# Down projection as seven block products, with two of the weight sums made by accumulating transfers

## The chip, the cores and the metric

The kernel runs on one core of a Trainium2 chip. The metric is the device time of one execution in microseconds; lower is better. TensorE multiplies and adds into PSUM, VectorE and ScalarE work on SBUF and PSUM, GpSimd on SBUF; SP issues nearly all transfers, each engine works through its own queue in order, and engines wait for each other by semaphores.

## The reference: what is computed

A decoder layer on 512 tokens of width 1024: RMSNorm, three token mixers (two of attention, one state space model) with gates, a projection back, a residual; then RMSNorm, a gated feed-forward with a short convolution, a residual, and a last RMSNorm. The change is in the feed-forward and the last norm:

```python
def conv_ffn(h, w_up, conv_w, conv_b, w_down):
    up = h @ w_up                                  # (512, 1024) @ (1024, 5632)
    up = conv_general_dilated(up, conv_w, ...) + conv_b   # 3 taps, per channel
    gate, val = split(up, 2)
    return (silu(gate) * val) @ w_down             # (512, 2816) @ (2816, 1024)
x = x + conv_ffn(rmsnorm(x, norm_ffn), ...)
out = rmsnorm(x, norm_final)
```

## The kernel before

All arithmetic is float32. TensorE multiplies in a shorter format, so each operand is split into a high part (a copy made by ScalarE into that format, L66) and a low part (the difference, made by VectorE, L92 for weights), and each product is three matmuls: high x high, high x low, low x high (`mm3m`, L177 to L179).

The order of all work is written by hand. `units` is a list of steps, each with the weight chunk that it uses; `run` goes through it, and before each step it emits the splits of the next chunk, whatever `plan` has for that step (`before(u, ...)`) and what the step before left in `later`. A chunk is loaded by SP into one of two `raw` buffers of 1 MB; its pieces of 128 x 1024 are split into `whi` and `wlo`, four buffers each, so a split waits for TensorE to be done with the piece four before it.

The up stage takes the 22 blocks of 128 channels two at a time, c = 0 to 10. For each c there are four steps of 24 matmuls (gate and value, two blocks each). ScalarE and VectorE do the convolution of each result in the tile `cc`, ScalarE the silu, VectorE the product; ScalarE and VectorE split the product into `gh[f]` and `gl[f]`, 128 channels x 512 tokens.

The down stage (`down_unit`) computes the output in two halves of 512 columns. In each it goes through the 22 channel blocks in six chunks (2, 4, 4, 4, 4, 4), with four accumulators in PSUM, one for each 128 tokens: 2 x 22 x 4 x 3 matmuls. When the first half ends, `residual` adds the four results to `x1`, ScalarE sums squares, and GpSimd multiplies by the final norm's weights (`gfin`). In the second half the accumulators end one after another; for the last 128 tokens the last four blocks are done in two pieces of 256 columns (`fin`), so that the end after the last matmul is short. `finish` makes the power -0.5 on GpSimd, scales the two halves on ScalarE and VectorE, and SP stores each.

Of the kernel before, what the change touches and what calls it, by code (L numbers as in the profile page):

```python
# [31 lines left out]
def hybrid_block(  # L32
# [167 lines left out]
    def run(first, live):  # L200
# [14 lines left out]

        def split_to(ci, n):
# [10 lines left out]
            if done[ci] == len(c.defs):  # L227
                load_to(ci + 3)
# [914 lines left out]
    gfin = []  # L1143

    def load_gfin():
        gfin.append(hp_.tile([128, DM], F32, tag="hTh", name="gfin"))
# [4 lines left out]
    def down_unit(chunk, half, k0, n):
        def fn():
            if k0 == 0:
                for t in range(NT):
                    acc[t] = bank(DTAG[half][t], name="acc")
            order = [(t, k) for k in range(n) for t in range(NT)]
            whole = slice(0, 512)
            if k0 + n == NF:
                order = [(t, k) for t in range(NT) for k in range(n)]
                if half == 1:  # L1160
                    order = order[:-n]
            order = [(t, k, whole) for t, k in order]
            final = k0 + n == NF and half == 1
            if final:

                order += [(NT - 1, k, c) for c in (slice(0, 256), slice(256, 512)) for k in range(n)]
                fin = {0: bank("sc", name="fin"), 256: bank("pt", name="fin")}
            for t, k, c in order:
                o = slice(t * 128, t * 128 + 128)
                kk = k0 + k  # L1170
                w = tuple(v[:, c] for v in chunk.get(k))
                if final and t == NT - 1:
                    ps, starts, stops = fin[c.start][:, 0:256], k == 0, k == n - 1
                else:
                    ps = acc[t]
                    starts, stops = kk == 0, kk == (NF - 5 if half == 1 and t == NT - 1 else NF - 1)
                mm3m(ps, gh[kk][:, o], gl[kk][:, o], w, starts, stops)
                if not stops:
                    continue
                if kk < NF - 1:  # L1180
                    y = x1[t // 2][:, t % 2, 512:1024]
                    tt(y, y, ps, ADD)
                    continue
                if half == 0:
                    residual(t, half, acc[t], fss)
                    row = x1[t // 2][:, t % 2, whole]
                    stt(fss[:, 8 + t:9 + t], fss[:, t:t + 1], 1.0 / DM, epsv, MUL, ADD)
                    tt(row, row, gfin[0][:, whole], MUL, G)
                    continue
                y, oc = x1[t // 2][:, t % 2, 512 + c.start:512 + c.stop], cc[0][:, t, c]  # L1190
                ss = fss[:, 4 + t:5 + t] if c.start == 0 else fss[:, 12:13]
                tt(y, y, ps, ADD)
                S.activation(ps, y, AF.Square, accum_out=ss)
                for f in rest[:1] if final and t == NT - 1 else rest[:]:
                    rest.remove(f)
                    f()
                tt(oc, y, gfin[0][:, 512 + c.start:512 + c.stop], MUL, G if t < NT - 2 else V)
                parts.append(ss)
                if c.stop == 512:
                    for ss in parts:  # L1200
                        ms = fss[:, 8 + t:9 + t]
                        stt(ms, ss, 1.0 / DM, ms, MUL, ADD)
                    parts.clear()
                    finish(t)
# [4 lines left out]
    def finish(t):
        ms, row, y = fss[:, 8 + t:9 + t], x1[t // 2][:, t % 2, 0:512], cc[0][:, t, :]  # L1210
        G.tensor_tensor(ms, ms, mhalf, op=ALU.pow)

# [4 lines left out]
        def second():
            ts(y, y, ms, MUL)
            SY.dma_start(out[0, t * 128:(t + 1) * 128, 512:1024], y)

        rest.extend((first, second))
# [195 lines left out]
```

## Time and profile before

| | before |
|---|---|
| median of 3 runs | 832.57 us (831.45 to 832.61) |
| profiled execution, its own time | 834.41 us |
| profiled execution, its span | 832.6 us |
| TensorE busy | 815.8 us, 98% |
| VectorE, ScalarE, GpSimd busy | 470.8, 363.3, 160.1 us |
| up stage, down stage | to 705.8 us, then to 825.6 us |

The span runs from the first to the last instruction that the profiler saw. A line number such as L92 is that of the source; where a helper issues an operation, it is the helper's. Matmuls overlap: one of 512 columns shows 389 ns, but the next starts earlier. "PEld" is TensorE's load of the stationary operand.

### The profile page before, as it was taken

The numbers are of one execution on the slowest core, as the hardware profiler recorded it, in microseconds if no ns is written. First come the engines' busy times: TensorE is split into PE (matmuls) and PEld (weight loads), VectorE is DVE, ScalarE is ACT, GpSimd is POOL, SyncE is SP. The second block draws the span as 40 slices with busy tenths as digits, with TensorE's granted clock in tenths as the row PEclk, the third lists the DMA queues.
The fourth block names the chain that finished last, engine by engine and source line by source line (L and its number), as shares of the span: only waits on it lengthen the run. The fifth ranks groups of instructions, "written<-read, shape, count | busy, mean of one in ns | idle before, by whom it ended". The sixth has DMA issues, their size and how long they took to land.

```text
span 832.6 us, 10517 instructions
## 1 busy us (share of the span) xinstructions
PE 815.8 (98%) x4085; PEld 677.2 (81%) x4085; DVE 470.8 (57%) x913; ACT 363.3 (44%) x673; POOL 160.1 (19%) x217
## 2 busy tenths in 40 slices
PE   8999899999999999999999999999999999999996
PEld 7978778778787888888878998888888888888885
DVE  7998666674636638272755466655566555423313
ACT  6446556457354546242443354444444444313212
POOL 6199623523200100032610000000000000002002
PEclk9999799999999999999999999999999999999998
DMA  9332131132331122332261313333333323412402
GB/s 248 96 103 62 40 102 52 51 95 46 63 106 52 53 78 76 102 102 70 93 245 51 99 52 102 101 102 102 101 102 102 101 77 102 167 60 77 152 0 102
DMA packets 68277, 76.60 MB, mean 92 GB/s; under 512 B 8160, under 2 KB 55556, under 8 KB 68228
## 3 DMA queue, kind: packets, MB, share of 16 engines
q1 hardware_dynamic: 67972, 75.89, 28.7%
q8 instruction: 32, 0.52, 0.3%
q0 software_dynamic: 256, 0.05, 0.1%
q14 instruction: 17, 0.14, 0.1%
HBM read 73.81 MB, written 2.12 MB: 91 GB/s over the span
## 4 chain that ended last, share of the span: by engine, by line
PE 84%; DVE 8%; DMA 2%; ACT 2%; issue 1%; POOL 1%; SPq 1%; POOLq 0%; DVEq 0%; ACTq 0%
PE mm L171 10%; PE up L172 10%; PE up L171 10%; PE up L173 10%; PE mm L172 9%; PE mm L173 9%; PE acc L178 6%; PE acc L179 6%; PE acc L177 6%; DVE wlo L92 1%; DVE us L624 1%; PE sc L895 1%; PE sc L763 1%; PE sc L684 1%; PE o L722 1%
## 5 line engine op out<-in xcount | busy, mean ns | idle before, releaser
L92 DVE TENSOR_TENSOR wlo<-raw,whi 128x1024 fp32r<-128x1024 f32 (+1 forms) x126 | 150.3, 1203 | 152.5 <-ACT whi L66 152.4
L66 ACT ACTIVATE whi<-raw 128x1024 fp32r<-128x1024 f32 (+1 forms) x126 | 127.3, 1023 | 58.4 <-PE acc L179 56.2
L171 PE MATMUL up<-hTh,whi 128*128 128x512 f32 (+1 forms) x384 | 142.7, 372 | 0.0
L172 PE MATMUL up<-hTl,whi 128*128 128x512 f32 (+1 forms) x384 | 142.6, 371 | 0.0
L173 PE MATMUL up<-hTh,wlo 128*128 128x512 f32 (+1 forms) x384 | 142.6, 371 | 0.0
L171 PE MATMUL mm<-hTh,whi 128*128 128x512 f32 (+1 forms) x336 | 133.5, 397 | 0.0
L172 PE MATMUL mm<-hTl,whi 128*128 128x512 f32 (+1 forms) x336 | 130.5, 388 | 0.0
L173 PE MATMUL mm<-hTh,wlo 128*128 128x512 f32 (+1 forms) x336 | 130.3, 388 | 0.0
L275 DVE SCALAR_TENSOR_TENSOR cc<-up,cpar,cc 128x511 f32<-128x511 f32 x88 | 65.9, 749 | 97.3 <-ACT cc L1107 95.8
L171 PEld LDWEIGHTS up<-hTh,whi 128*128 128x128 f32 x384 | 72.3, 188 | 12.6
L173 PEld LDWEIGHTS up<-hTh,wlo 128*128 128x128 f32 x384 | 72.3, 188 | 12.5
L172 PEld LDWEIGHTS up<-hTl,whi 128*128 128x128 f32 x384 | 72.3, 188 | 12.3
L171 PEld LDWEIGHTS mm<-hTh,whi 128*128 128x128 f32 x336 | 64.2, 191 | 14.7 <-issue 2.5
L173 PEld LDWEIGHTS mm<-hTh,wlo 128*128 128x128 f32 x336 | 63.9, 190 | 13.1
L172 PEld LDWEIGHTS mm<-hTl,whi 128*128 128x128 f32 x336 | 63.9, 190 | 11.8
L178 PE MATMUL acc<-wlo,gh 128*128 128x512 f32 x172 | 66.9, 389 | 0.0
L179 PE MATMUL acc<-whi,gl 128*128 128x512 f32 x172 | 66.9, 389 | 0.0
L177 PE MATMUL acc<-whi,gh 128*128 128x512 f32 x172 | 66.9, 389 | 0.0
L279 POOL TENSOR_TENSOR x<-x,gfin 128x512 f32<-128x512 f32 x4 | 5.2, 1290 | 296.8 <-ACT acc L1046 296.8
L1107 ACT ACTIVATE cc<-up,cpar 128x512 f32<-128x512 f32 x44 | 34.3, 779 | 61.2 <-PE up L173 60.4
L989 ACT ACTIVATE th<-mm 128x512 f32<-128x512 f32 x24 | 14.3, 595 | 67.3 <-PE mm L173 67.3
L66 ACT ACTIVATE gh<-cc 128x512 fp32r<-128x512 f32 x22 | 13.9, 632 | 59.4 <-DVE cc L279 59.4
(297 smaller groups left out, 1271.4 us busy)
## 6 DMA issues: line engine op xcount, KB each, us to landing
raw<-in_w_up_dram SPq DMA_DIRECT2D x22, 1024.0 KB, 5.1
raw<-in_w_in_dram SPq DMA_DIRECT2D x18, 1024.0 KB, 5.1
raw<-in_w_down_dram SPq DMA_DIRECT2D x10, 1024.0 KB, 5.0
x<-in_x_dram SPq DMA_DIRECT2D x8, 512.0 KB, 6.1
raw<-in_w_in_dram SPq DMA_DIRECT2D x8, 512.0 KB, 5.4
raw<-in_w_out_dram SPq DMA_DIRECT2D x4, 1024.0 KB, 5.0
raw<-in_w_branch_a_dram SPq DMA_DIRECT2D x4, 512.0 KB, 5.9
raw<-in_w_branch_c_dram SPq DMA_DIRECT2D x2, 1024.0 KB, 5.0
```

The source lines that it names most:

```text
L66: S.activation(o, i, AF.Copy)
L92: (lo_eng or V).tensor_tensor(view(lo), r, view(hi).bitcast(F32), op=ALU.subtract)
L171: PE.matmul(ps, wh, xh, start=first, stop=False)
L172: PE.matmul(ps, wh, xl, start=False, stop=False)
L173: PE.matmul(ps, wl, xh, start=False, stop=last)
L177: PE.matmul(ps, xh, wh, start=first, stop=False)
L178: PE.matmul(ps, xh, wl, start=False, stop=False)
L179: PE.matmul(ps, xl, wh, start=False, stop=last)
L275: emit(lambda: V.scalar_tensor_tensor(o, a, s, b, op0=op0, op1=op1))
L624: V.tensor_copy(US[j][32 * tau:32 * tau + 32], uT[0][32 * j:32 * j + 32].rearrange("p t (c a) -> p t c a", a=4)[:, :, :, tau])
L989: S.activation(t, ps, AF.Tanh, scale=0.5)
L1107: S.activation(dst, ps, AF.Identity, bias=cpar[:, 3, f:f + 1], scale=cpar[:, 2, f:f + 1])
```

## The change

With the tokens, the channels and the output columns each cut into two halves, the product of 2 x 2 by 2 x 2 blocks is made of seven block products, p1 to p7, in place of eight. A half of the tokens is 256 (tiles 0, 1 and tiles 2, 3). A half of the channels is every second block: block 2c + j is row j of pair c, so a product runs over 11 pairs. Each product has a token part (a block or a sum of blocks of the gated values) and a weight part (a block or a sum of blocks of `w_down`).

- **Token parts.** In the up stage `sums` forms them for each c from the tile of values: part 1 (for p1 and p5) is split at once, part 2 (p6, p4) at once for c < 5, parts 3 (p2, p3), 4 (p7) and the other parts 2 are left as sums. `late` splits those in the down stage, at steps given by a table. The dictionaries `gh` and `gl` go.
- **Weight parts.** `Sum` is a chunk for one product and a group of two pairs (or the one pair 10): 512 KB loaded by SP into one of six half-size buffers (four in the two `raw` tiles, two in `big`, in the place of the up stage's input). For p5 and p7 GpSimd then issues a second transfer that adds another 512 KB of `w_down` to it as it lands (`accum_op=ADD`). For p6 and p4 VectorE adds the raw tile of the product before (`sum`), between the high and the low part of another block. Up to three blocks are split ahead.
- **Order.** 42 steps, numbered 0 to 41 here. The first sweep (0 to 23) goes through six groups of pairs, (0,1), (2,3), (4,5), (10), (6,7), (8,9), with p1, p5, p6, p4 in each. The second (24 to 41) has p2, p7, p3 for the first four groups, then p7 twice, p2 twice, p3 twice for the last two. A step is 2 token tiles x pairs x 3 matmuls.
- **Results.** `ends` puts each finished product where it belongs: into `x2`, a copy of `x1`, or into `es`, which sums p1 and p6 for the right half; `slow` spreads the rest of that sum over steps 25 to 30. `x1` is stored to DRAM early in the up stage (`park`) and comes back as `x2` in the down stage (`down_loads`, before step 9, with `gfin`), since its place holds token parts meanwhile. The pieces of 256 columns at the end go.

```diff
+    class Sum:
+        def load(self):
+            self.raw = raw_tile(self.nk)
+            SY.dma_start(self.raw, self.block(self.col, self.row))
+            if self.acc:
+                G.dma_start(self.raw, self.block(*self.acc), accum_op=ADD)
+        def sum(self):
+            if self.plus is not None and not self.acc and not self.summed:
+                V.tensor_tensor(self.raw, self.raw, self.plus.raw, op=ADD)
+            self.summed = True
+        def split(self, i, hi_eng=None, lo_eng=None):
+            r = self.raw
+            self.sum()
+            hi, lo = (piece([128, 2, 512], n)[:, 0:self.nk, :] for n in ("whi", "wlo"))
+            copy_act(hi, r)
+            if self.next is not None and self.next.raw is not None:
+                self.next.sum()
+            V.tensor_tensor(lo, r, hi.bitcast(F32), op=SUB)
+            self.p[0] = (hi, lo)
...
             if done[ci] == len(c.defs):
-                load_to(ci + 3)
+                load_to(ci + (6 if isinstance(c, Sum) else 3))
...
             tt(v, v, g, MUL)
-            gh[f], gl[f] = slot([128, T], F32R, name="gh"), slot([128, T], F32R, name="gl")
-            copy_act(gh[f], v)
-            later.append(lambda: tt(gl[f], v, gh[f][:, :].bitcast(F32), SUB))
+            if a:
+                later.append(lambda: sums(c))
...
+    def sums(c):
...
+        v = cc[0][:, 2:4, :]
+        a11, a12, a21, a22 = (v[:, j, t * 256:t * 256 + 256] for t in range(2) for j in range(2))
+        s5 = s6 = a21
+        tt(R[c - c % 2, 4][:, Q1 if c % 2 else Q0], a11, a21, SUB)
+        tt(s5, a21, a22, SUB)
+        parts((c, 1), v[:, 0, :])
+        tt(s6, s5, a11, SUB)
+        two = lambda t: t.rearrange("p (j n) -> p j n", j=2)
+        if c < FULL:
+            parts((c, 2), v[:, :, Q1], two)
+        else:
+            R[c, 2] = store(F32)
+            copy_act(two(R[c, 2]), v[:, :, Q1])
+        R[c, 3] = store(F32)
+        copy_act(R[c, 3][:, Q0], a12)
+        tt(R[c, 3][:, Q1], a12, s6, ADD)
+
+    def late(c, i):
+        o = Q0 if (c, i) == (NP - 1, 4) else slice(0, T)
+        parts((c, i), R.pop((c, i))[:, o], lambda t: t[:, o])
...
+    def ends(kind, t):
+        ps = PS[kind, t]
+        if kind == "p1":
+            es[t] = slot([128, 512], name="e")
+            copy_act(es[t], ps)
+            add_to(t, 0, ps)
+        elif kind == "p6":
+            tt(es[t], es[t], ps, ADD)
+            add_to(2 + t, 0, es[t])
+        elif kind == "p4":
+            e, p5 = es[t], PS["p5", t]
+            add_to(2 + t, 0, ps)
+            slow.extend((lambda: tt(e, p5, e, SUB), lambda: add_to(t, 1, e), lambda: add_to(2 + t, 1, e)))
...
+        elif kind == "p7":
+            add_to(2 + t, 0, ps)
+            add_to(2 + t, 1, ps, SUB)
+            square(2 + t, 0, ps)
+            square(2 + t, 1, ps)
+            part(2 + t, 0)
+            finish(2 + t)
...
-    for half in range(2):
-        k0 = 0
-        for n in (2, 4, 4, 4, 4, 4):
-            ch = krows(w_down[0], k0, n, half * 512)
-            add(ch, down_unit(ch, half, k0, n))
-            k0 += n
...
+        for d, key in enumerate(fs[::-1]):
+            before(u_down + 24 + 3 * min(gi, 4) - 3 + d + (gi == 5), lambda k=key: late(*k))
```

Three places where the queues change. First GpSimd, from the out projection (`ssq`) to the end. Before, it has nothing in the up stage and, in the down stage, the products with `gfin` and the powers:

```order
L331 TENSOR_TENSOR ssq<-ssq,mhalf 128x1 x4
L279 TENSOR_TENSOR x_3896<-x_3896,gfin 128x512 x2
L279 TENSOR_TENSOR x_3897<-x_3897,gfin 128x512 x2
L279 TENSOR_TENSOR cc<-x_3896,gfin 128x512
L1211 TENSOR_TENSOR fss<-fss,mhalf 128x1
```

The same place after; `raw` and `big` are the weight buffers, 128x2x512 is half a MB:

```order
L370 TENSOR_TENSOR ssq_151<-ssq_151,mhalf_77 128x1 x4
L185 DMA raw_5800<-in_w_down_dram 128x2x512
L185 DMA big_5989<-in_w_down_dram 128x2x512
L185 DMA raw_5913<-in_w_down_dram 128x2x512
L185 DMA raw_5800<-in_w_down_dram 128x512
```

Twelve accumulating transfers stand there now, ahead of all of the powers and products.

Second VectorE where one half of the down stage follows on the other. Before: the four results of the first half, then the splits of the second.

```order
L92 TENSOR_TENSOR wlo<-raw,whi 128x1024 x7
L279 TENSOR_TENSOR x_3896<-x_3896,acc 128x512
L275 SCALAR_TENSOR_TENSOR fss<-fss,epsv 128x1
...
L279 TENSOR_TENSOR x_3897<-x_3897,acc 128x512
...
L92 TENSOR_TENSOR wlo<-raw,whi 128x1024 x10
```

After, from the results of p1 (step 20) on; the three `wlo` are the blocks of steps 24, 25 and 26, the three `op` are `late` subtractions, of which the last, op_6442, belongs to step 24:

```order
L318 TENSOR_TENSOR x2_5988<-x2_5988,p1_5998 128x512
L200 TENSOR_TENSOR wlo_6390<-raw_5800,whi_6389 128x1024
L318 TENSOR_TENSOR op_6395<-op_4523,op_6394 128x512
L200 TENSOR_TENSOR wlo_6411<-raw_5800,whi_6410 128x1024
L318 TENSOR_TENSOR op_6416<-op_4685,op_6415 128x512
L318 TENSOR_TENSOR e_6377<-e_6377,p6_6045 128x512
L318 TENSOR_TENSOR x2_5988<-x2_5988,e_6377 128x512
L318 TENSOR_TENSOR e_6386<-e_6386,p6_6052 128x512
L318 TENSOR_TENSOR x2_5988<-x2_5988,e_6386 128x512
L200 TENSOR_TENSOR wlo_6436<-raw_5913,whi_6435 128x1024
L318 TENSOR_TENSOR op_6442<-op_4535,op_6441 128x512
```

Splits, token parts and results now take turns there.

Third VectorE at the end. Before, after the last split:

```order
L279 TENSOR_TENSOR x_3897<-x_3897,fin 128x256
L269 TENSOR_SCALAR cc<-cc,fss 128x512
L279 TENSOR_TENSOR cc<-x_3897,gfin 128x256
L275 SCALAR_TENSOR_TENSOR fss<-fss 128x1 x2
L269 TENSOR_SCALAR cc<-cc,fss 128x512
```

After, from the split of step 40 (wlo_6731) to the sum of p3's first tile (step 41):

```order
L200 TENSOR_TENSOR wlo_6731<-big_5989,whi_6730 128x1024
L318 TENSOR_TENSOR x2_5988<-x2_5988,p7_6492 128x512 x2
...
L314 SCALAR_TENSOR_TENSOR x2_5988<-x2_5988,fss_152,big_5989 128x512 x2
L318 TENSOR_TENSOR x2_5988<-x2_5988,p7_6499 128x512 x2
...
L314 SCALAR_TENSOR_TENSOR x2_5988<-x2_5988,fss_152,big_5989 128x512 x2
L200 TENSOR_TENSOR wlo_6769<-big_5989,whi_6768 128x1024
L318 TENSOR_TENSOR x2_5988<-x2_5988,p2_6468 128x512
L314 SCALAR_TENSOR_TENSOR fss_152<-fss_152,epsv_78 128x1
L318 TENSOR_TENSOR x2_5988<-x2_5988,p2_6475 128x512
...
L318 TENSOR_TENSOR x2_5988<-x2_5988,p3_6517 128x512
```

The last split (wlo_6769, for step 41) stands behind the whole of p7's results.

## Rows read from the trace of the kernel before

**Rows 1.** busy time of the page, then its chain that ended last by engine

```profile
PE 815.8 (98%) x4085; PEld 677.2 (81%) x4085; DVE 470.8 (57%) x913; ACT 363.3 (44%) x673; POOL 160.1 (19%) x217
...
PE 84%; DVE 8%; DMA 2%; ACT 2%; issue 1%; POOL 1%; SPq 1%; POOLq 0%; DVEq 0%; ACTq 0%
```

**Rows 2.** stretches: us, busy (count) by engine, PEclk, DMA share, GB/s

```profile
640.00:680.00 40.00, 40.00 (x178) 33.10 (x178) 23.01 (x29) 17.73 (x24) 0.00 (x0) 1.00 0.32 105
715.00:730.00 15.00, 15.00 (x68) 12.43 (x67) 5.03 (x5) 3.18 (x3) 0.00 (x0) 1.00 0.51 177
790.00:805.00 15.00, 15.00 (x68) 12.43 (x67) 2.45 (x2) 3.18 (x3) 0.00 (x0) 1.00 0.00 0
```

**Rows 3.** tile acc: ns min/median/max, first and last start

```profile
L177 PE MATMUL acc<-whi,gh x172: 389/389/390, 705.8 to 822.1; 128*128 128x512 f32 x172
```

**Rows 4.** timeline of the end, by engine: start, us, operation

```profile
825.50 0.28 PE L179 MATMUL fin<-whi,gl 128*128 128x256 f32 x1
...
824.55 0.15 DVE L275 SCALAR_TENSOR_TENSOR fss<-fss 128x1 f32<-128x1 f32 x1
824.63 0.41 DVE L279 TENSOR_TENSOR x<-x,fin 128x256 f32<-128x256 f32 x1
...
827.97 0.48 DVE L269 TENSOR_SCALAR cc<-cc,fss 128x512 f32<-128x512 f32 x1 [0.66 <-POOL fss L1211]
...
827.38 0.55 POOL L1211 TENSOR_TENSOR fss<-fss,mhalf 128x1 f32<-128x1 f32 x1 [2.05 <-DVE fss L275]
...
829.14 0.38 SPq L1219 DMA_DIRECT2D out_dram<-cc  x1
```

**Rows 5.** waits in 680 to 833: us in total, times, longest

```profile
ACT whi L66 <- PE acc L179: 56.2, 14, 4.4
DVE wlo L92 <- ACT whi L66: 54.9, 16, 4.2
```

**Rows 6.** groups by shape in 680 to 833: busy us, mean ns

```profile
L275 DVE SCALAR_TENSOR_TENSOR cc<-up,cpar,cc 128x511 f32<-128x511 f32 x6 | 4.5, 750 | 14.7 <-ACT cc L1107 14.7
...
L279 DVE TENSOR_TENSOR gl<-cc,gh 128x512 fp32r<-128x512 f32 x4 | 2.7, 685 | 0.0
...
L1193 ACT ACTIVATE acc<-x 128x512 f32<-128x512 f32 x3 | 1.8, 596 | 13.3 <-DVE x L279 13.3
...
L1046 ACT ACTIVATION_READ_ACCUMULATOR acc<-x 128x1 f32 x4 | 0.7, 187 | 0.0
```

**Rows 7.** timeline of VectorE, then ScalarE, work in a row

```profile
708.26 2.35 DVE L92 TENSOR_TENSOR wlo<-raw,whi 128x1024 fp32r<-128x1024 f32 x2
710.52 0.68 DVE L279 TENSOR_TENSOR gl<-cc,gh 128x512 fp32r<-128x512 f32 x1
711.12 0.69 DVE L279 TENSOR_TENSOR cc<-cc 128x512 f32<-128x512 f32 x1
...
712.38 1.99 ACT L66 ACTIVATE whi<-raw 128x1024 fp32r<-128x1024 f32 x2
```

**Rows 8.** transfers: KB each, us to landing; then that of x

```profile
raw<-in_w_down_dram SPq DMA_DIRECT2D x2, 512.0 KB, 3.3
...
d<-nlB POOLq DMA_DIRECT2D x2, 8.0 KB, 2.3
...
DMA to landing us min/median/max: 7.4/7.7/8.1
```

**Rows 9.** timeline of TensorE; then stretches, columns as in rows 2

```profile
86.89 1.64 PE L763 MATMUL sc<-pj 64*128 64x128 f32 x8 [2.25 <-DVE mxA L770]
...
94.92 0.63 PE L171 MATMUL mm<-hTh,whi 128*128 128x512 f32 x1
95.35 0.63 PE L172 MATMUL mm<-hTl,whi 128*128 128x512 f32 x1
...
87.00:87.50 0.50, 0.50 (x4) 0.40 (x6) 0.26 (x4) 0.00 (x0) 0.50 (x2) 0.61 0.00 0
...
123.00:124.00 1.00, 0.05 (x1) 0.05 (x1) 1.00 (x6) 0.51 (x1) 0.71 (x1) 1.00 0.00 0
```

More of the change, by code (lines that the diff above doesn't have):

```diff
@@ L212, in load_to @@
             while state["loaded"] < min(n, len(order)):
+                if isinstance(order[state["loaded"]], Sum) and rn[0] >= 4 and not RB:
+                    return
                 order[state["loaded"]].load()
@@ L1141, in up_unit @@
         return fn
-    gfin = []
-    def load_gfin():
-        gfin.append(hp_.tile([128, DM], F32, tag="hTh", name="gfin"))
-        SY.dma_start(gfin[0], norm_final[None, :].to_broadcast([128, DM]))
-    DTAG = (("sc", "sc", "pt", "pt"), ("mm", "mm", "o", "o"))
-    def down_unit(chunk, half, k0, n):
-        def fn():
[L1153 to L1204, printed above, removed]
-        return fn
@@ L1207, in hybrid_block, with park, down_begin @@
-    parts, rest = [], []
+    gfin, x2, RS, RB, RW, rn = [], [], [], [], [], [0]
+    xd = dr.tile([T, DM], F32, tag="xd", bufs=1, name="xd")
+    def park():
+        for t in range(NT):
+            SY.dma_start(xd[t * 128:(t + 1) * 128, :], x1[t // 2][:, t % 2, :])
+    def down_begin():
+        x2.append(hp_.tile([128, NT, DM], F32, tag="hTh", name="x2"))
+        big = hp_.tile([128, 4, DM], F32, tag="hTl", name="big")
+        gfin.append(big[:, 0, :])
+        RS.append(big[:, 1, 0:512])
+        RB.extend(big[:, j, :] for j in (2, 3))
@@ new lines, in hybrid_block, with xv, add_to, square @@
+    PS = {}
+    BANK = {"p1": "sc", "p5": "pt", "p6": "mm", "p4": "o", "p2": "sc", "p7": "mm", "p3": "o"}
+    def xv(t, half):
+        return x2[0][:, t, half * 512:half * 512 + 512]
+    def add_to(t, half, ps, op=ADD):
+        tt(xv(t, half), xv(t, half), ps, op)
+    def square(t, half, junk):
+        S.activation(junk, xv(t, half), AF.Square, accum_out=fss[:, 2 * t + half:2 * t + half + 1])
+    def down_unit(chunk, kind, k0, n, first, last):
+        def fn():
+            for t in range(2):
+                if first:
+                    PS[kind, t] = bank(BANK[kind], name=kind)
+                for k in range(n):
+                    xh, xl = (v[:, t * 128:t * 128 + 128] for v in tok(k0 + k, kind))
+                    mm3m(PS[kind, t], xh, xl, chunk.get(k), first and k == 0,
+                         last and k == n - 1)
+                if last:
+                    ends(kind, t)
+        return fn
@@ L1209, in finish, with part @@
+    slow = []
+    es = {}
+    def part(t, half):
+        ms, ss = fss[:, 8 + t:9 + t], fss[:, 2 * t + half:2 * t + half + 1]
+        stt(ms, ss, 1.0 / DM, epsv if half == 0 else ms, MUL, ADD)
     def finish(t):
-        ms, row, y = fss[:, 8 + t:9 + t], x1[t // 2][:, t % 2, 0:512], cc[0][:, t, :]
+        ms = fss[:, 8 + t:9 + t]
+        part(t, 1)
         G.tensor_tensor(ms, ms, mhalf, op=ALU.pow)
-        def first():
-            copy_act(row, row, scale=ms)
-            SY.dma_start(out[0, t * 128:(t + 1) * 128, 0:512], row)
@@ L1217, in second @@
[L1217 to L1221, printed above, removed]
-        if t == NT - 1:
-            first()
-            second()
-        elif t < NT - 2:
-            rest.pop(0)()
+        if t < 2:
+            tt(xv(t, 1), xv(t, 1), gfin[0][:, 512:], MUL)
+            ts(xv(t, 1), xv(t, 1), ms, MUL)
+            copy_act(xv(t, 0), xv(t, 0), scale=ms)
+        for half in (1, 0):
+            o = slice(half * 512, half * 512 + 512)
+            if t >= 2:
+                stt(xv(t, half), xv(t, half), ms, gfin[0][:, o], MUL, MUL)
+            SY.dma_start(out[0, t * 128:(t + 1) * 128, o], xv(t, half))
@@ L1385, in hybrid_block @@
     before(u_up + 2, lambda: norm2(1, ("pt", "sc", "pt", "sc")))
-    before(u_down + 1, load_gfin)
+    before(u_up + 3, park)
+    before(u_down, down_begin)
+    before(u_down + 9, down_loads)
     run(cu[1], 2)
```

87 lines of the change are left out of this document (86 added, 1 removed).

## The prediction

> **What bounds the kernel now.** I read the busy table first: TensorE is busy for 98% of the span, and the chain that ended last runs over it for 84% [rows 1]. The table by stretch then says what lies beside it. In the up stage (640 to 680) VectorE has 23.0 us of work in 40; in the down stage (from 705.8) it has 2.5 to 5.0 in 15, ScalarE 3.2, and the clock stands at full speed throughout [rows 2]. So the down stage is pure TensorE time: of 3 x 172 matmuls of 512 columns the first of each three start between 705.8 and 822.1 [rows 3], which is 116.3 / (171 x 3) = 0.2267 us from one matmul to the next, without a gap. Last I read the tail: the last matmul starts at 825.50, VectorE's last operation at 827.97, the last output transfer is issued at 829.14, and the span ends 3.5 us later at 832.6 [rows 4]. The splits wait for TensorE to free their buffers and not the other way round: 54.9 us of VectorE's waiting is for high parts, and 56.2 us of ScalarE's is for TensorE [rows 5]. Whatever takes matmuls away here shortens the kernel, as long as weights, token parts and the tail keep up.
>
> **Part 1, fewer matmuls.** Before: 516 x 0.2267 + 24 half-width ones at 0.12 = 119.9 us (705.8 to 825.6). After: 7 products x 11 pairs x 2 token tiles x 3 = 462 matmuls of 512 columns, 104.7 us. **-15.1 us.** A step of two pairs is then 12 matmuls, 2.72 us; a step of pair 10 alone is 1.36.
>
> **Part 2, the up stage.** For each c, `sums` puts in place of two `gl` subtractions (0.69 each [rows 6]) four of 256 columns and one or two of 512. Where VectorE works without a pause, two splits take 2.35, so 1.14 each, and operations of 512 columns follow each other by 0.60 [rows 7]; one of 256 took 0.41 [rows 4], so they follow by about 0.34. VectorE gets at most 1.4 us more in each 21.8 us, where it idles 9. ScalarE gets a copy of 256 columns. The four stores of `park` move 2 MB on SP's queue beside w_up loads that keep the transfer engines a third busy [rows 2]. I cost all this at nothing; if the cover were gone it would be 11 x 1.4 = 15 us.
>
> **Part 3, weights in the down stage.** Every step now needs a weight block of its own: 42 splits for 22. I call it by its step. VectorE's share of four steps (10.9 us) holds 4 splits, 2 sums of 1024 columns and up to 2 `late` subtractions: 6 x 1.14 + 1.2 = 8.0 us; ScalarE has 4 x 0.95 + 1.1 [rows 7]. That fits, with the lead of three steps that four split buffers give. Transfers: 177 GB/s took 0.51 of the engines [rows 2], so they move 347 GB/s and half a MB (0.524 MB) costs 1.5 us of all of them. Four loads are 6.0 us per 10.9 in the first sweep, three are 4.5 per 8.2 in the second, each with one accumulating transfer more.
>
> No row shows an accumulating transfer. Its nearest rows are the plain 512 KB load, 3.3 us from issue to landing, and the tiny transfer issued by GpSimd, 2.3 us [rows 8]. From below it is like a plain one, 2.3 + 1.5 = 3.8 us; nothing makes it cheaper. From above, let it cost the engines twice a plain one, for what it brings and what it adds to, and share them with two loads queued beside it: 2.3 + 3 + 3 = 8.3; the queue that fetched `x` behind other loads shows such a length, 7.4 to 8.1 [rows 8]. I take 6.5. It bites first at step 5 (`p5` of the second group). The load goes to a tile that TensorE frees only when the up stage ends. It is second in the queue, so it lands 3.3 + 1.5 + 0.3 = 5.1 us after that. The sum and the split behind it end 2.4 us after the accumulate lands, and TensorE wants the low part at 5 x 2.72 + 0.23 = 13.8. So up to 6.3 us is free; at 8.3 it costs 2.0, at 6.5 it costs 0.2. The second place is `down_loads`: 2.6 MB (7.5 us of all engines) go into SP's queue ahead of blocks 18 to 21, which also stops the accumulate for block 21. I get 0 to 1.5 us there and take 1.0. **Together +1.2 us** (0 to 3.5).
>
> The Trainium skill (DMA: Bandwidth & Descriptors, Anatomy of one DMA) fits a transfer issued by GpSimd as 2.0 us + bytes / 436e3, by which half a MB would land in 3.2 us, and this term would be 0. Against it stands the Trainium skill's Collectives: The Full Stack, section The bandwidth ceiling, where an add in the transfer engine costs twice a copy since both operands are read, which would leave it about where I put it. No row here shows which holds.
>
> **Part 4, the boundary of the sweeps.** `p2` of group 0 (step 24) needs the third token part of pair 0, whose low half stands in VectorE's queue behind the splits of blocks 24, 25 and 26, two other `late` subtractions and the results of `p1` and `p6` (the order after the change, above). Counted from the start of step 21: the split of block 24 can end at 3.0 (its buffer is free at 0.2, ScalarE copies the results of `p1` until 0.8, then 1.05 for the high part and 1.2), then 0.6; block 25, 1.14, and 0.6, which makes 5.7; four sums of the `p6` results, 2.5; the split of block 26, 1.14; the wanted subtraction, 0.69: 10.1. Step 24 starts at 8.15 and its third matmul wants that part at 8.6. **+1.5 us**; queued behind VectorE's row are the later splits, and I count them just in time for steps 27 and 30 (0.2 us to spare). The same rows bound it: with all of the sums waiting (6 results at 0.69) it is 3, with the results done earlier it is 0.
>
> **Part 5, the tail.** Let E be the end of the last matmul without further stalls. VectorE works without a pause from the start of step 33 (E - 20.4): from 1.2 us later five splits and six `late` subtractions take 5.7 + 3.6 and end at E - 9.9. Then come the results of `p7`. For each of two tiles: two sums 1.3, the square of the second 0.8 (0.60 + 0.19 [rows 6]), the two small ones 0.3, GpSimd's power 0.6 [rows 4], two products 1.4 (the 511-column form takes 0.75 [rows 6]); 4.4 each. So the split of block 41, queued behind them, ends at E - 9.9 + 8.7 + 1.2 = E. TensorE wanted it at E - 2.5, and so stops for some 2.5 us. After the split: `p2`, two times (0.65 + 0.79 + 0.16), 3.2; `p3` tile 0, sum 0.65, square 0.8, small 0.2, product 0.6, scale 0.45 = 2.7; tile 1 the same to the scale's own end, 2.9; the last issue and landing 0.4 + 3.5. The span ends at E + 12.7. Before it is 832.6 - 825.6 = 7.0. **+5.7 us.** TensorE's stop costs nothing on top, since VectorE's row is longer.
>
> **The sum.** -15.1 + 1.2 + 1.5 + 5.7 = -6.7, taken as -6.6. The profiled execution took 834.41 with a span of 832.6, 1.8 of it outside; so it would be 827.8. The median of the runs shown is 832.57, and becomes **826.0 us**.
>
> **Rivals.**
> *A, the accumulates starve TensorE (slower than before).* Let one cost X us of all engines. The first sweep then needs 6.0 + X per 10.9 us, the second 4.5 + X per 8.2; there are 5.5 such rounds in each. Over both, TensorE would lose 5.5 x (2X - 8.6), less some 8 us by which the loads run ahead. It eats the gain of 6.6 from X = 5.6 on; X = 6 costs 10.7, some 837, and X = 7 21.7, some 848. For it: half a MB plain is 1.5 us and no row says what the sum in the engine costs. Against it: it would have to be over three and a half times the plain price.
> *B, latency at two places only.* The accumulate lands in 8 to 10 us at step 5, and the 2.6 MB in front of block 18 cost 3: +4 to +6, 829 to 832.
> *C, the clock.* After 2.25 us without a matmul the granted clock went from 1.0 to 0.5 (2.4 to 1.2 GHz) at 87, and at 95 matmuls are still 0.43 apart [rows 9]. At 123 TensorE was busy for 0.05 us of one microsecond, and the clock stayed at 1.0 [rows 9]. If the stop of 1.5 us at the boundary does it, ten microseconds at half speed cost up to 4.8, 828 to 831. At the end it costs nothing, by part 5.
> *D, a shorter tail.* If the results of `p7` and `p2` overlap better than I chained them (VectorE's waits for squares and powers are 6 x 0.8 + 4 x 0.6 of it), 3 us less: 822 to 823.
> *E, the matmuls are not fewer.* The program issues 462 of them; this rival is empty, but their gain could be given back in the up stage (15 us, part 2). That gives some 841, with 1%.
>
> **How the numbers follow.** Forecast with its own range 823.5 to 829: 0.53. A 0.15, B 0.14, C 0.09, D 0.08, E 0.01. The range 822.5 to 832.5 leaves out A, E and half of D. About 0.2% (1.7 us) is what a measurement of this kernel can tell from no change: the forecast, C, D and a third of B lie under 830.9, 0.75; the rest of B and a sliver of A within, 0.10; slower 0.15.
>
> **What would show it.** In the profile after: 462 matmuls in the down stage; a wait of TensorE at the first `p2`, for VectorE, of 1 to 2 us; another of 2 to 3 us at the last `p3`, for a low part; 12 to 13 us from the last block's nominal end to the end of the span, with VectorE on the chain; issue to landing of the accumulates under 8 us; transfers 0.6 to 0.9 busy. It is wrong if TensorE waits for transfers in every group (A), or if the tail is at 7 us.

## The result: 14 us slower, where 6.6 us faster was forecast

| | before | after |
|---|---|---|
| median | 832.59 us (831.45 to 834.29) | 846.58 us (845.57 to 847.25) |
| ratio | | 1.0165 (1.0144 to 1.0187) |
| span of the profiled execution | 832.6 us | 845.4 us |
| down stage: first matmul, end of the last | 705.8, 825.6 | 704.8, 837.1 |

Of all executions used below, one (of run e5) took 2808 us and is left out; every other lies within 1.5% of its kernel's fastest.

The page of the kernel after: busy times, the transfer queues (packets, MB, share of 16 engines' span), and the chain that ended last.

```profile
PE 810.6 (96%) x4007; PEld 668.1 (79%) x4007; DVE 538.1 (64%) x1018; ACT 393.5 (47%) x725; POOL 169.5 (20%) x225
...
q1 hardware_dynamic: 73780, 88.74, 32.3%
q0 software_dynamic: 3264, 5.82, 4.1%
...
PE 73%; DVE 10%; DMA 9%; ACT 3%; issue 2%; POOL 1%; SPq 0%; POOLq 0%; ACTq 0%; DVEq 0%
```

Against [rows 1], TensorE is busy for 5 us less and yet for a smaller share, and transfers hold 9% of the chain in place of 2%. The stretches (columns as in [rows 2]):

```profile
640.00:680.00 40.00, 40.00 (x178) 33.14 (x177) 26.14 (x36) 18.79 (x26) 0.00 (x0) 1.00 0.30 100
...
705.00:720.00 15.00, 13.60 (x60) 10.92 (x59) 9.44 (x13) 5.64 (x8) 1.26 (x2) 1.00 0.90 278
...
735.00:755.00 20.00, 19.58 (x87) 15.89 (x86) 11.53 (x15) 7.78 (x11) 1.39 (x2) 1.00 0.97 326
...
775.00:790.00 15.00, 9.91 (x32) 7.67 (x33) 11.40 (x16) 5.99 (x9) 2.33 (x2) 0.77 0.82 196
```

The up stage is whole (40.00 of 40). In the down stage, TensorE stands still at several places while the transfer engines are 0.8 to 1.0 busy, and no compute engine is full. How long a transfer takes from issue to landing there (median; L183 on SP's queue is the load, L185 on GpSimd's the accumulate):

```profile
raw<-in_w_down_dram SPq DMA_DIRECT2D x23, 512.0 KB, 7.0
big<-in_w_down_dram SPq DMA_DIRECT2D x12, 512.0 KB, 5.1
...
raw<-in_w_down_dram POOLq DMA_DIRECT2D x7, 512.0 KB, 8.4
...
big<-in_w_down_dram POOLq DMA_DIRECT2D x3, 512.0 KB, 9.4
```

The quiet load of [rows 8] took 3.3. Step 5 in the timeline (all engines, order of time):

```profile
710.18 1.22 POOL L185 DMA_DIRECT2D big<-in_w_down_dram  x1 [22.08 <-DMA big<-in_w_down_dram]
...
718.21 0.39 PE L216 MATMUL p<-whi,op 128*128 128x512 f32 x1
...
719.59 1.23 DVE L189 TENSOR_TENSOR raw<-raw,big 128x1024 f32<-128x1024 f32 x1 [3.87 <-DMA big<-in_w_down_dram]
...
719.66 1.06 ACT L66 ACTIVATE whi<-big 128x1024 fp32r<-128x1024 f32 x1 [3.44 <-DMA big<-in_w_down_dram]
...
720.77 0.54 PE L214 MATMUL p<-whi,op 128*128 128x512 f32 x1 [2.18 <-ACT whi L66]
...
722.03 0.80 PE L215 MATMUL p<-wlo,op 128*128 128x512 f32 x1 [0.72 <-DVE wlo L200]
...
722.63 0.63 PE L216 MATMUL p<-whi,op 128*128 128x512 f32 x1
...
723.05 0.63 PE L214 MATMUL p<-whi,op 128*128 128x512 f32 x1
```

The accumulate for block 5 was issued at 710.18 and landed at 719.6, 9.4 us later. ScalarE, VectorE and TensorE wait for it one after the other, and then the matmuls start 0.43 apart: the granted clock is 0.51 between 721 and 727 and 1.00 again between 728 and 733. The boundary of the sweeps:

```profile
764.95 1.20 POOL L185 DMA_DIRECT2D raw<-in_w_down_dram  x1 [8.93 <-DMA raw<-in_w_down_dram]
...
773.47 1.06 ACT L66 ACTIVATE whi<-raw 128x1024 fp32r<-128x1024 f32 x1 [2.51 <-DMA raw<-in_w_down_dram]
...
773.66 0.39 PE L216 MATMUL p<-whi,op 128*128 128x512 f32 x1
...
774.43 0.61 ACT L66 ACTIVATE op<-op 128x512 fp32r<-128x512 f32 x1
...
775.90 0.61 ACT L66 ACTIVATE op<-op 128x512 fp32r<-128x512 f32 x1
...
776.57 0.50 PE L214 MATMUL p<-whi,op 128*128 128x512 f32 x1 [2.52 <-ACT op L66]
...
780.09 0.68 DVE L318 TENSOR_TENSOR op<-op 128x512 fp32r<-128x512 f32 x1
...
780.83 0.80 PE L216 MATMUL p<-whi,op 128*128 128x512 f32 x1 [3.53 <-DVE op L318]
```

At 773.47 ScalarE had waited for the accumulate of block 25 (issued at 764.95). Behind this high part, in the same in-order queue, stand the copies of token parts that step 24 wants, and behind these VectorE's subtractions. So a block that is wanted one step later stops TensorE twice. It would itself have been in time: it was split by 775.8, and without the stops TensorE would have wanted it at 776.6.

### The profile page after: what moved, and what is told of

It is laid out like the page before. It is cut to its first block, busy times and chain, and to the rows that moved or that the text cites. A ratio compares the mean times of both kernels' runs of the same rounds, so it can differ in the third digit from the quotient of the medians.

```text
span 845.4 us, 10648 instructions
## 1 busy us (share of the span) xinstructions
PE 810.6 (96%) x4007; PEld 668.1 (79%) x4007; DVE 538.1 (64%) x1018; ACT 393.5 (47%) x725; POOL 169.5 (20%) x225
## 3 DMA queue, kind: packets, MB, share of 16 engines
q0 software_dynamic: 3264, 5.82, 4.1%
## 4 chain that ended last, share of the span: by engine, by line
PE 73%; DVE 10%; DMA 9%; ACT 3%; issue 2%; POOL 1%; SPq 0%; POOLq 0%; ACTq 0%; DVEq 0%
PE mm L208 10%; PE up L209 10%; PE up L210 9%; PE up L208 9%; PE mm L210 9%; PE mm L209 9%; DMA raw<-in_w_down_dram 5%; DMA big<-in_w_down_dram 2%; DVE wlo L200 1%; DVE us L663 1%; PE p L216 1%; PE acc L215 1%; PE p L215 1%; PE acc L216 1%; ACT whi L66 1%
## 5 line engine op out<-in xcount | busy, mean ns | idle before, releaser
L92 DVE TENSOR_TENSOR wlo<-raw,whi 128x1024 fp32r<-128x1024 f32 (+1 forms) x104 | 123.1, 1193 | 94.5 <-ACT whi L66 94.4
L66 ACT ACTIVATE whi<-raw 128x1024 fp32r<-128x1024 f32 (+1 forms) x132 | 131.7, 1008 | 35.4 <-DMA raw<-in_w_down_dram 13.9
L214 PE MATMUL p<-whi,op 128*128 128x512 f32 x146 | 60.1, 412 | 8.4 <-ACT whi L66 5.9
L185 POOL DMA_DIRECT2D raw<-in_w_down_dram x8 | 9.4, 1172 | 276.6 <-DVE wlo L92 221.1
L215 PE MATMUL p<-wlo,op 128*128 128x512 f32 x146 | 60.6, 415 | 3.8 <-DVE wlo L200 3.8
L216 PE MATMUL p<-whi,op 128*128 128x512 f32 x146 | 60.3, 413 | 4.2 <-DVE op L318 4.2
L1028 ACT ACTIVATE th<-mm 128x512 f32<-128x512 f32 x24 | 14.3, 595 | 65.5 <-PE mm L210 65.4
L214 PEld LDWEIGHTS p<-whi,op 128*128 128x128 f32 x146 | 29.1, 199 | 16.6 <-ACT whi L66 7.2
```

What stands on the lines that cost most here:

```text
L66: S.activation(o, i, AF.Copy)
L92: (lo_eng or V).tensor_tensor(view(lo), r, view(hi).bitcast(F32), op=ALU.subtract)
L185: G.dma_start(self.raw, self.block(*self.acc), accum_op=ADD)
L214: PE.matmul(ps, xh, wh, start=first, stop=False)
L215: PE.matmul(ps, xh, wl, start=False, stop=False)
L216: PE.matmul(ps, xl, wh, start=False, stop=last)
```

## The experiments

What TensorE lost is worked out from the starts of the 462 matmuls of each profiled execution: the distance from one to the next less 0.2267 us [rows 3], added up over steps. It holds both stops and the slow clock behind them. In us; "behind" is from the last matmul's end (its start plus 0.2267) to the end of the span. Steps 0 to 4 lost nothing in any of them.

| kernel | median (ratio to before, 95%) | span | down stage from | 5-9 | 10-17 | 18-23 | 24-35 | 36-41 | behind |
|---|---|---|---|---|---|---|---|---|---|
| after | 846.58 (1.0144-1.0187) | 845.4 | 704.8 | 6.2 | 0.7 | 2.2 | 9.4 | 9.0 | 8.3 |
| e1 no accumulates | 826.41 (0.9908-0.9945) | 826.1 | 704.8 | 0.1 | 0 | 0 | 2.1 | 6.1 | 8.3 |
| e2 copied, not added | 830.93 (0.9963-0.9990) | 826.7 | 703.1 | 0.3 | 1.1 | 0.2 | 2.8 | 5.6 | 8.8 |
| e3 token parts earlier | 843.32 (1.0109-1.0144) | 842.3 | 704.6 | 4.1 | 3.2 | 3.0 | 7.0 | 7.3 | 8.6 |
| e4 block 41 ahead of p7 | 845.66 (1.0132-1.0182) | 844.6 | 704.1 | 6.5 | 1.3 | 2.5 | 9.0 | 0.5 | 16.0 |
| e5 accumulates of 1/8 | 831.92 (0.9977-1.0005) | 830.1 | 706.0 | 0.1 | 0 | 0 | 4.9 | 5.7 | 8.7 |
| e6 other loads of 1/8 | 830.47 (0.9961-0.9984) | 828.8 | 703.3 | 3.7 | 0 | 0.2 | 2.5 | 5.5 | 8.9 |
| e7 sums on VectorE | 834.29 (1.0005-1.0030) | 832.9 | 703.9 | 1.1 | 1.1 | 0.2 | 6.3 | 7.3 | 8.3 |
| e8 sums on GpSimd | 841.23 (1.0079-1.0119) | 838.9 | 703.0 | 6.4 | 0 | 1.0 | 8.3 | 7.2 | 8.3 |
| e9 earlier loads | 841.64 (1.0090-1.0120) | 840.4 | 706.0 | 3.8 | 2.1 | 1.8 | 7.8 | 5.7 | 8.7 |
| e10 e9 + order | 834.99 (1.0015-1.0044) | 830.3 | 704.2 | 0.7 | 3.4 | 0.9 | 5.1 | 0 | 11.3 |
| e11 e7 + order | 831.33 (0.9968-0.9997) | 829.1 | 704.5 | 1.1 | 1.2 | 0.1 | 5.9 | 0 | 11.5 |
| e12 sums in the up stage | 827.22 (0.9924-0.9959) | 824.9 | 703.3 | 0.1 | 0 | 0 | 2.1 | 5.5 | 9.2 |
| e13 e12 + order | 822.90 (0.9867-0.9903) | 822.7 | 706.0 | 0.1 | 0 | 0 | 0.4 | 0 | 11.6 |

The start of the down stage moves by up to 3 us between executions of kernels whose up stage is the same (after and e1 to e11: 703.0 to 706.0); I count it as no effect of the edits. The program has twelve accumulating transfers, ten of 512 KB and two of 256; where expectations say eleven or nine, twelve and ten are meant.

**e1, the accumulates left out.**

```diff
-                G.dma_start(self.raw, self.block(*self.acc), accum_op=ADD)
```

> Leaves out the 11 accumulating transfers, so the blocks of p5 and p7 hold one of their two weight blocks; everything else stands as in the changed kernel. Theory W (the accumulating transfers land late: the waits for blocks 5, 20, 21, 25, 36 and 37 and the slow clock behind them are theirs): block 5's 2.9 us and 3.2 us of half clock, 1.8 at blocks 20 and 21, the boundary's 6.0 less what VectorE's order alone costs there (1.5) and its 3 us of clock, 2.5 at the tail, together -15: 830 to 834. Theory Q (the order in VectorE's and ScalarE's queues at the boundary and in the tail is what costs): the boundary and the tail stay, only block 5 goes: 839 to 842. Theory M (SP's loads and the 2.6 MB of down_loads are late by themselves): 843 to 847.

826.4: 20.2 us less than after, more than theory W gave. The table says where: 19.2 of it are stops and slow clock, in steps 5 to 41; nothing else changed. What is left at the boundary:

```profile
766.16 0.68 DVE L318 TENSOR_TENSOR op<-op 128x512 fp32r<-128x512 f32 x1
...
766.90 0.50 PE L216 MATMUL p<-whi,op 128*128 128x512 f32 x1 [1.56 <-DVE op L318]
```

This is the stop of 1.5 that part 4 foretold, from VectorE's order alone. It leaves the clock at full speed.

**e2, the same transfers without the sum.**

```diff
-                G.dma_start(self.raw, self.block(*self.acc), accum_op=ADD)
+                G.dma_start(self.raw, self.block(*self.acc))
```

> The second transfer of each pair overwrites the block instead of adding to it, so the sum is left out; count, queue, issue and bytes of the transfers stay. If what costs is the second read inside the transfer engines (some 3.0 us of all engines against 1.5), the landing falls from 8.4 to 9.4 us to 5 to 7 and the time to 834 to 839. If what costs is that a transfer issued by GpSimd stands behind the hardware queue's loads whatever it does, the landing stays at 8 us or more and the time at 844 to 847.

830.9, less than the 834 to 839 of the first theory, and the queue and the landings of this kernel's page:

```profile
q0 software_dynamic: 1856, 5.82, 2.3%
...
raw<-in_w_down_dram POOLq DMA_DIRECT2D x7, 512.0 KB, 4.0
...
big<-in_w_down_dram POOLq DMA_DIRECT2D x3, 512.0 KB, 7.5
```

Less the 0.1% that the queue had before the change (0.8 us), it holds all engines for 2.3% x 826.7 - 0.8 = 18.2 us; with the sum 4.1% x 845.4 - 0.8 = 33.9. That is 11 half MB: **1.65 us copied, 3.1 us added** (the shares are rounded, so each holds to some 0.05). The same 5.82 MB took 3264 packets with the sum and 1856 without. The sum, and not the second transfer, makes 16 of the 20 us.

**e3, group 0's late token parts four steps earlier; e4, p7's results one step later.**

```diff
-            before(u_down + 24 + 3 * min(gi, 4) - 3 + d + (gi == 5), lambda k=key: late(*k))
+            before(u_down + 24 + 3 * min(gi, 4) - (3 if gi else 7) + d + (gi == 5), lambda k=key: late(*k))
...
-                    ends(kind, t)
+                    if kind == "p7":
+                        later.append(lambda t=t: ends(kind, t))
+                    else:
+                        ends(kind, t)
```

> Nothing left out; the late token parts of group 0 are made four steps earlier, ahead of the splits of blocks 24 and 25 in ScalarE's and VectorE's queues. Theory Q: the two stops at the boundary (2.52 and 3.53) and the 3 us of half clock behind them go, -6 to -9: 838 to 841. Theory W: block 25's landing is what is late; with the token parts ahead of it step 24 runs but step 25 then waits for its own block, -2 to -4: 842 to 845. Theory V (VectorE has no room before step 20, splits of blocks 21 to 23 become late): no change or +1 to +3: 846 to 850.

> Nothing left out; the results of p7 are emitted one step later, so that the split of block 41 stands ahead of them in VectorE's and ScalarE's queues. Theory Q: TensorE's stop before the last product (3.12 and 1.95, and its half clock) goes; VectorE's row from 821 to 841 keeps its length, so the end moves by 1 to 3 only: 843.5 to 845.5. Theory P (TensorE's stop is what sets the end): -5 to -7: 839.5 to 841.5. Theory W (blocks 36 and 37, landed at 812, set the start of VectorE's row, and the order behind it is worth nothing): 846 to 847.

e3: 843.3, theory W's range, but not by its mechanism: step 25 does not wait for its own block. Step 24 no longer stops, and step 27 stops for 2.9 and 1.4, since its token part stands in ScalarE's queue behind the high part of block 28, whose accumulate landed at 782.56. The same tie has moved on by one round. e4: 845.7, at the edge of Q. The stop before the last product is gone (9.0 to 0.5), and nearly all of it comes back behind the last matmul (8.3 to 16.0): as part 5 said, VectorE's row sets the end, not TensorE.

**e5, accumulates of 64 columns in place of 512; e6, the other loads of 64 columns.** In e6 the blocks without an accumulate keep most of what their buffer held.

```diff
-                G.dma_start(self.raw, self.block(*self.acc), accum_op=ADD)
+                G.dma_start(self.raw[:, :, 0:64], self.block(*self.acc)[:, :, 0:64], accum_op=ADD)
```

```diff
-            SY.dma_start(self.raw, self.block(self.col, self.row))
+            n = 512 if self.acc or rn[0] <= 6 else 64
+            SY.dma_start(self.raw[:, :, 0:n], self.block(self.col, self.row)[:, :, 0:n])
```

> Each accumulating transfer brings 64 of its 512 columns, so seven eighths of each sum are left out; count, queue, order of issue and waits stay. Theory X (what costs is the time of the transfer engines, 3.0 us for half a MB of adding): an eighth of it is some 0.4 us, the landing falls to 3 to 4 us and the time to that of the kernel without accumulates, 826 to 828. Theory L (a fixed latency: a second, dependent transfer in a chain of load, sum, split): landing 4 to 5, time 829 to 833.

> Behind the first six, the plain loads of blocks that have no accumulate bring 64 of 512 columns (so most of those weights are left out); the accumulates and their own loads stay whole. Theory X (the accumulates are late because they share the engines with four and three loads per round, 6.0 + 3.0 us of 10.9): with that work gone an accumulate lands in some 5 us as where it stood alone, the stops at the boundary, at blocks 20, 21 and 36, 37 go, block 5's stays (its neighbours are whole), 831 to 836. Theory S (an accumulate lands in 8 to 9 us by itself): landing unchanged, 842 to 846.

e5: 831.9, the time of theory L, though the stops at steps 5, 17 and 21 went as X said. Its `raw` transfers land in 3.2, its `big` ones, though just as short, in 6.1: there even 64 KB from GpSimd wait some 3 us longer. Of the 5.5 above e1 the profiles place 2.8 at the boundary and 1.2 in the start of the down stage; the rest is that e1's profiled execution (827.90) lay 1.5 above its median. e6: 830.5, just under the range of theory X. The accumulates are as large as ever, but land sooner:

```profile
raw<-in_w_down_dram POOLq DMA_DIRECT2D x7, 512.0 KB, 5.7
big<-in_w_down_dram POOLq DMA_DIRECT2D x3, 512.0 KB, 7.9
```

The `big` ones still begin beside whole transfers, which held 0.74 to 1.00 of the engines until their first packet. Only step 5, whose neighbours are whole, still stops, besides the boundary and the tail. The packets of the kernel after say the same: the accumulate for block 1, alone in the up stage, had its first packet 0.7 us after its issue ended and moved for 3.4; that for block 5 waited 1.7 and moved for 6.1, with 0.48 of the engines held by loads meanwhile. So the cost needs both: the sum's 3.1 us and busy engines beside it.

**e7, the sums on VectorE; e8, on GpSimd** (from the raw tiles of p1 and p3, which lie in SBUF; the last two p7 keep their accumulates).

```diff
-            ch.acc = {"p5": (0, 0), "p7": (1, 1)}.get(kind)
+            ch.acc = {"p7": (1, 1)}.get(kind) if k0 in (6, 8) else None
...
+            if kind == "p7" and not ch.acc:
+                ch.plus = group["p3", k0]
```

```diff
+            for c in [self] + sums_of.get(self, []):
+                if c.gsum and c.raw is not None and c.gsum.raw is not None and not c.summed:
+                    G.tensor_tensor(c.raw, c.raw, c.gsum.raw, op=ADD)
...
```

> Nothing left out: 9 of the 11 accumulating transfers are undone, and VectorE adds the weight blocks of p1 and p3, which lie in the raw tiles anyway, into those of p5 and p7; the accumulates of the last two p7 stay. It adds a sum of 1.2 us to VectorE's 8 us in each round of 10.9. Theory X: 826 to 830, with the boundary's stop as in the kernel without accumulates or 1 to 2 us longer. Theory V (VectorE, now with 9.2 of 10.9, becomes the bound): stops of the low parts in every round, 832 to 838.

> Nothing left out: the same nine sums by GpSimd instead of VectorE, when the later of the two loads has been issued. Theory X: 826 to 829, since GpSimd is idle there. Theory G (a GpSimd sum of 1024 columns takes several us and slows VectorE beside it): 831 to 838.

e7: 834.3, the range of theory V, though TensorE stops at steps 5, 17, 24 and 41 and not in every round. VectorE is full ahead of the boundary, 19.52 us of 20 (columns as in [rows 2]: TensorE, its weight loads, VectorE):

```profile
755.00:775.00 20.00, 16.07 (x64) 12.80 (x63) 19.52 (x24) 9.34 (x13) 0.00 (x0) 0.91 0.60 184
```

e8: 841.2, worse than theory G. In the timeline one GpSimd sum and the VectorE operation beside it:

```profile
768.83 2.79 POOL L190 TENSOR_TENSOR big<-big 128x1024 f32<-128x1024 f32 x1 [4.60 <-DMA big<-in_w_down_dram]
...
769.30 2.86 DVE L325 TENSOR_TENSOR op<-op 128x512 fp32r<-128x512 f32 x1
```

That subtraction takes 0.68 elsewhere; here it is done half a microsecond after GpSimd is. Step 5, which loses 6.4, shows the same: two VectorE subtractions of 128 x 512 took 2.89 and 2.60 beside GpSimd sums of 3.38 and 2.39, and the split of block 5 stands behind them in the queues.

**e9, a block with an accumulate is loaded one place earlier; e10 and e11, that and e7 with the order changed.** The order: e3's edit, and in the tail the results of both tiles together. Conditions are shortened.

```diff
+        for i in range(1, len(loads)):
+            while loads[i].acc and not loads[i - 1].acc and ...:
+                loads[i - 1:i + 1] = [loads[i], loads[i - 1]]
```

```diff
         elif kind == "p7":
...
-            part(2 + t, 0)
-            finish(2 + t)
+            fin.append(lambda: (part(2 + t, 0), power(2 + t)))
+            done_.append(lambda: finish(2 + t))
...
+        if t == 1:
+            fs = fin + done_
...
+            if kind == "p7":
+                later.extend(fs)
```

> Nothing left out; only the order of the loads changes: a block that gets an accumulate is loaded one place earlier (block 37 two places), ahead of a block that gets none. Transfers, bytes and sums stay. Theory R (round trip: a raw buffer comes round after 6 steps, 16.3 us, and load plus issue plus accumulate plus split take 7.0 + 1.2 + 8.4 + 2.4 = 19.0): the accumulates gain 2.7 us of lead, most stops at blocks 5, 20, 21 and 25 go, 833 to 839. Theory E (the transfer engines lack the throughput, whatever the order): 844 to 848.

> As the run before, and besides: group 0's late token parts four steps earlier, and in the tail the results of p7, p2 and p3 emitted for both tiles at once (sums of both tiles, then the split of block 41, then the small operations and products), so that VectorE need not wait for each square and power in turn. From the run before, theory Q (VectorE's order holds 2 to 6 us at the boundary and 5 to 7 in the tail): -6 to -10, 824 to 831. If the tail's length is work and not waits: -2 to -4, 831 to 837.

> Sums by VectorE as in the run with nine accumulates undone, with the late token parts four steps earlier and the tail in the order of the run before. From 834.3: the boundary's stop of 4.3 us with 2 us of slow clock behind it goes, and the tail's waits, 5 to 7: 821 to 824. If VectorE is full at the boundary, the stop only moves: 826 to 829.

e9: 841.6, between R and E. More lead helps at step 5 (6.2 to 3.8) and not at 17 (0.7 to 2.1). There the low part stands in VectorE's queue behind the sum of block 18, and the load of that block, issued 1.4 us later than before, landed at 750.17, behind the 2.6 MB of `down_loads`. e10: 6.7 below e9, the difference that Q gave, though not the time (its profiled execution was its fastest, others lie up to 837.7); its boundary stops at step 27, as in e3. e11: 3.0 below e7, neither of the two: the tail is 4.1 shorter, but the boundary's stop moved from step 24 to 27; VectorE is full ahead of it (19.86 us of 20).

**e12, all twelve sums made in the up stage, in device memory; e13, that with the order of e10.**

```diff
+        def presum(self):
+            self.pre = dr.tile([128, self.nk, 512], F32, ...)
+            SY.dma_start(self.pre, self.block(self.col, self.row))
+            G.dma_start(self.pre, self.block(*self.acc), accum_op=ADD)
...
-            SY.dma_start(self.raw, self.block(self.col, self.row))
-            if self.acc:
+            SY.dma_start(self.raw, self.pre if self.pre is not None else self.block(self.col, self.row))
+            if self.acc and self.pre is None:
...
+            if ch.acc:
+                before(u_up + 3 * len([1 for _, c in sums_ if c.acc]), ch.presum)
```

> Nothing left out: each of the 12 sums that an accumulating transfer makes is made in the up stage, where the transfer engines are 0.3 busy: a plain copy of one weight block from device memory to device memory, an accumulate onto it, and in the down stage one plain load of the sum. Bytes and accumulates rise by 12 copies of 0.5 MB. Theory P (an accumulate costs by where it stands, behind a load of its own and in a stage where the engines are 0.7 to 1.0 busy): as the kernel without accumulates, 825 to 829. Theory U (copies between device memory, 12 x 4.5 us of all engines, delay the loads of the up stage, where TensorE has no gap so far): 830 to 845.

> As the run before, with group 0's late token parts four steps earlier and the tail's results emitted for both tiles at once. Against the run before, by what the same two moves did to the sums by VectorE (3.0 less) and to the changed order of loads (6.7 less): -3 to -7, so 819 to 825 under theory P. If VectorE's row is what sets the end there: -1 to -3, 823 to 828.

e12: 827.2, theory P. The transfers are more by 6 MB, and yet all the accumulates' stops are gone. A stretch of its up stage, and the landing of its accumulates:

```profile
500.00:540.00 40.00, 40.00 (x178) 33.14 (x177) 26.94 (x37) 16.56 (x22) 2.93 (x3) 1.00 0.56 139
...
pre<-in_w_down_dram POOLq DMA_DIRECT2D x10, 512.0 KB, 6.1
```

The transfer engines are 0.56 busy (0.26 in the kernel after), and TensorE works for 40.00 of 40. e13: **822.9 us, 1.15% faster than before**, and the fastest version that leaves nothing out. It lies 4.3 below e12, within the 3 to 7 expected from the two moves. Its down stage in two stretches:

```profile
706.00:756.00 50.00, 50.00 (x222) 41.37 (x221) 40.77 (x46) 26.60 (x34) 0.00 (x0) 1.00 0.78 273
756.00:811.00 55.00, 55.00 (x243) 44.97 (x241) 45.72 (x63) 29.03 (x43) 1.08 (x2) 1.00 0.42 134
```

No stop is left: 462 matmuls in 105.2 us.

## Why the prediction was wrong, point by point

In spans it said -6.7; measured +12.8, and -6.5 in e1. That e1 meets the forecast is in part luck: there the start of the down stage and the weights give back 2.1 of what the boundary and the tail cost more. By its terms:

| term | predicted | after | without accumulates (e1) |
|---|---|---|---|
| start of the down stage | 0 | -1.0 | -1.0 |
| 1, matmuls | -15.1 | -15.1 | -15.1 |
| 2, up stage | 0 | 0 | 0 |
| 3, weights (steps 5 to 23) | +1.2 | +9.2 | +0.1 |
| 4, boundary (24 to 35) | +1.5 | +9.4 | +2.1 |
| 5, tail, from E, less 7.0 | +5.7 | +10.2 | +7.3 |
| sum | -6.7 | +12.7 | -6.6 |

E is the end of the matmuls with all losses up to step 35; in the kernel after 704.84 + 104.73 + 18.57 = 828.1, and the span ends 17.2 later.

**Part 1 and part 2** were right: 0.2267 us per matmul, 40.00 of 40 in the up stage.

**Part 3** is the step that failed, and not by its price: X was guessed at about 3 and is 3.1. What it had wrong is the time from issue to landing, taken as 6.5 with 8.3 as its upper end: the medians are 8.4 and 9.4, single ones reach 11.2. That end counted two loads beside the accumulate; a round has four or three, and they are themselves late (7.0 and 5.1, where I reckoned with 3.3). The slow clock behind a stop (2.9 us at step 5) was put at nothing.

And I asked at two places only. At step 5 the load landed 4.8 us after the up stage's end (foretold 5.1), and the accumulate was what came late. `down_loads`, taken as 1.0, cost 2.9 in steps 17 to 23 together with the accumulates (e1, without them, loses nothing there): the loads of blocks 18 and 21 landed 13.0 and 8.9 us after their issue. The question was, for every block that gets an accumulate, the time from its load's issue through the sum's landing and 2.4 us of split, against the time from there until TensorE wants the block. Read from the trace of the kernel after: 16.8 against 13.2 us at block 5, 20.2 against 18.3 at 21, 18.3 against 18.0 at 37; blocks 9, 28 and 31 took 15.6 to 16.9, had 24 to 27 and did not stop. The sum of medians in e9's expectation, 19.0 against a ring's turn of 16.3, is no such test: it counts the issue's 1.2 twice, as 8.4 begins with the issue, and blocks are split up to three steps ahead. e9 bears the question out in part only, since what is loaded earlier makes something else late.

The Trainium skill (Collectives: The Full Stack, The bandwidth ceiling) says of the reduce step in a ring of cores that its add needs two source reads, and so runs at half the rate of a copy. e2 agrees for this transfer: 3.1 against 1.65. By the other page that the prediction weighed, the Trainium skill (DMA: Bandwidth & Descriptors, Anatomy of one DMA), half a MB from GpSimd lands in 3.2 us; the plain copies of e2 took 4.0 to 7.5 beside the loads and the sums 8.4 to 9.4, so here the measurement decides, and the fit is no price for a busy stage.

**Part 4** had its mechanism right: e1 shows it alone, 1.7 at the stop. (Its pieces 3.0, 0.6, 1.14 and 0.6 make 5.3 and not 5.7, so they give +1.1 and not +1.5.) What it missed is that ScalarE's queue ties step 24 to the landing of block 25: +7.3, of which 2.8 is slow clock (9.2 in steps 24 to 29, less 2.7 + 3.7 in the two stops).

**Part 5** was right in that VectorE's row sets the end (e4) and mis-sized by 1.6, which e1's timeline of VectorE shows:

```profile
801.95 1.28 DVE L318 TENSOR_TENSOR x<-x,p 128x512 f32<-128x512 f32 x2
804.02 0.16 DVE L314 SCALAR_TENSOR_TENSOR fss<-fss,epsv 128x1 f32<-128x1 f32 x1 [0.79 <-ACT p L1278]
804.77 0.16 DVE L314 SCALAR_TENSOR_TENSOR fss<-fss 128x1 f32<-128x1 f32 x1 [0.59 <-ACT p L1278]
...
811.90 1.22 DVE L200 TENSOR_TENSOR wlo<-big,whi 128x1024 fp32r<-128x1024 f32 x1
...
821.88 0.48 DVE L308 TENSOR_SCALAR x<-x,fss 128x512 f32<-128x512 f32 x1 [0.44 <-POOL fss L1335]
```

The row begins at E - 9.8 (foretold E - 9.9), but the results of p7 take 9.95 and not 8.7. The prediction let the first square of each tile run beside the second sum; in the trace it began at 803.26, after both sums, so VectorE waited for both squares, 0.79 and 0.59, in each of the two tiles. The rest is some 0.4 more in p2 and p3. In the kernel after, 2.9 come on top: the accumulate for block 37 landed 11.2 us after its issue, and VectorE's row begins later by that. In e13 the same work, with both tiles together, ends 11.6 behind the last matmul, 2.8 less than e1's 14.3 from E.

**The rivals.** A's threshold (5.6) was not reached; the engines were 0.87 busy from 705 to 755 and 0.83 from 755 to 811, and single transfers were late. B was nearest: 9.4 us at step 5, and 2.9 of its 3 at `down_loads`; the slow clock, the boundary and block 37 are not in it. C's price, up to 4.8, was 2.9 at step 5 (6.2 less 2.3 + 1.0 in the two stops) and 2.8 at the boundary; the prediction gave it to a stop that leaves the clock alone (1.56 us in e1, and so did one of 2.29 in e2). D did not come: the tail was longer, and only the other order takes some off, 2.8 in e13.

## What to carry to other kernels

An accumulating transfer is cheap where transfer engines are idle and dear where a buffer must take a load, a sum and a split one after the other: price the whole chain under load, each link at its loaded duration, against the time from the load's issue until the block is wanted, for every block and not at two places. Work that waits for a transfer delays whatever stands behind it in the same engine's queue, so a late block should not stand ahead of an operand that is wanted sooner. When weights are summed, a stage that leaves the transfer engines idle can do it ahead into device memory.

## What was not expected of the hardware

- Half a MB added by a transfer holds all engines for 3.1 us, copied 1.65; landed after 8.4 to 9.4 (medians; single ones 5.4 to 11.2) beside loads, 5.7 with little beside it (e6, `raw`), and in 6.1 in the up stage of e12.
- A GpSimd sum of 128 x 1024 took 2.38 to 3.38 us, and one VectorE subtraction beside it 2.86 in place of 0.68 (e8).
- Stops of 2.18 and 0.72 us, whose ends lie 1.3 apart, were followed by some 6 us at a granted clock of 0.51 (1.2 GHz); single ones of 1.56 us (e1) and 2.29 us (e2) left it at 1.0 (2.4 GHz).
